# Both MLPs of a two-layer diffusion transformer with seven products of quarters in place of eight

## Chip, cores and metric

The kernel runs on one core of one Trainium2 chip, in one launch. The metric is the device time of that core in microseconds (us): the median of several executions. All arithmetic is fp32 in accuracy: each matrix product is made of three TensorE matmuls on operands split in a high and a low fp32r part (high x high, low x high, high x low).

## What is computed

Two blocks of a transformer over 256 prompt tokens and 1024 latent tokens, width 1024. Layer 0 mixes tokens with a state-space scan and gated linear attention, layer 1 with softmax attention. Behind each mixer stands an MLP of hidden width 4096 with a squared ReLU:

```python
def sq_relu_mlp(h, w1, w2):
    return jnp.square(jax.nn.relu(h @ w1)) @ w2
...
hp = modulate(rms_norm(yp, norm_mlp[i]), sp2, cp2)
hs = modulate(rms_norm(ys, norm_mlp[i]), sl2, cl2)
yp = yp + gp2 * sq_relu_mlp(hp, w_mlp_in[i], w_mlp_out[i])
ys = ys + gl2 * sq_relu_mlp(hs, w_mlp_in[i], w_mlp_out[i])
```

## The kernel before

Activations lie transposed, features on partitions: 8 tiles of 128 features by tokens. The tokens are three blocks: tb 0 and tb 1 are 512 latent tokens each, tb 2 is the 256 prompt tokens. A scheduler puts the instructions of each engine in an order of its own from the order in which the code issues them, and slower side work (the norms, the modulation vectors) is threaded into the main stream by `tick` and `drain`. Tiles come from pools and rings, and PSUM banks from a ring for each use (`ps`): whoever takes a bank or a slot waits for its last reader.

`mixer_out` finishes the mixer: for each of 8 output tiles m it multiplies by the output weights (`dense`, L406 to L408, three matmuls for each of the contraction's tiles), adds the gated result to x (`upd`, L1240) and sums squares for the norm. `norm` makes the columns of inverse roots and then, tile by tile, the normed activation and its high and low part (L1273 on DVE, L393 on ACT, L394 on DVE, L395 on POOL or DVE).

`mlp` goes over 16 slices of 256 hidden features. For each slice `up` makes two hidden tiles of each token block (8 contraction tiles by 3 matmuls at L406 to L408, squared ReLU on ACT at L1366 and L1367, the split by DVE L1368 and POOL L1369), and `down` multiplies them by the two rows of the second weight matrix for all 8 output tiles (L1383 to L1385), each result added to x at once by `upd` on DVE. A latent block's matmul has a moving operand of 512 columns, the prompt block's one of 256. Weights come as loads of 512 KB from SP's queue (`wload`, L240), are rounded to the high part on ACT (L241) and their low part is subtracted on POOL (L242).

The second layer's modulation vectors (`adaln`, L275) are computed inside the MLP of layer 0.

Of the kernel before, what the change touches and what calls it, by code (L numbers as in the profile page):

```python
# [33 lines left out]
class Arena:  # L34
# [339 lines left out]
def acts(h):  # L374
    return lambda k: (h[k // 4][0][k % 4], h[k // 4][1][k % 4])
# [727 lines left out]
def gla_second(s, hm):  # L1103
# [209 lines left out]
def mixer_out(s, l, w_src, key, part, h, ready, half=False):  # L1313


    acc = {}
    a, b = s.AB[key], s.mod[l][:, part]
    wsrc = w_src.rearrange("(k p) m -> p k m", p=128)

    def one(m, tb, w):  # L1320
        n = TBS[tb][1]
        if m == 0:
            acc[tb] = sums(s, tb)
        if half:
            p = dense(s, w, 4, lambda k: acts(h[tb])(4 + k), n, off=128 * (m % 2), ms=256)
        else:
            p = dense(s, w, KT, acts(h[tb]), n)
        upd(s, p, l, 2, m, tb, xk(s, tb, m), acc[tb])

    def load(m, eng=None):  # L1330
        if not half:
            s.wm = wload(s, wsrc[:, :, 128 * m:128 * m + 128], eng=eng)
        elif m % 2 == 0:
            s.wm = wload(s, wsrc[:, 4:8, 128 * m:128 * m + 256])
        return s.wm

    ready(0)
    for m in range(8):
        one(m, 0, load(m, s.nc.vector if m < 4 else None))
    ready(1)  # L1340
    for m in range(8):
        w = load(m)
        one(m, 1, w)
        if m == 0:
            norm_side(s, 0, acc[0], a, b, h)
        one(m, 2, w)
    return lambda tb: norm_side(s, tb, acc[tb], a, b, h)
# [679 lines left out]
```

## Time and profile before

| quantity | value |
|---|---|
| median of three runs | 3386.04 us (3375.12 to 3386.8) |
| profiled execution, its own time | 3382.89 us |
| its span from first to last instruction | 3381.1 us |
| mean granted TensorE clock | 0.973 |
| PE busy | 3208.6 us (95%) |
| DVE busy | 1709.7 us (51%) |
| ACT busy | 1035.0 us (31%) |
| POOL busy | 1053.1 us (31%) |
| mean DMA rate | 80 GB/s |

The span is the time that the rows below fill; the 1.8 us between it and the execution's own time lie around it. A PE that is 95% busy says that the matmuls set the time in most stretches. The MLPs lie from about 762 to 1727 us (layer 0) and from about 2480 to 3369 us (layer 1).

### The profile page before, as it was taken

To read this page: it belongs to the slowest core of one execution; us is meant where nothing else is said; L and a number is where in the kernel's file an instruction comes from. 1 tells how busy PE (TensorE), PEld (TensorE's weight loads), DVE (VectorE), ACT (ScalarE), POOL (GpSimd) and SP (SyncE) were. 2 spreads that over 40 slices of the span, in tenths; PEclk is the share of its full clock that TensorE was granted. 3 is DMA by queue.
4 is the path that set the end of the run, shared out by engine and by line. 5 is a ranking of instruction groups with operands and counts; after the bars stand their busy time and mean duration, and the time that the engine had idled before them with its cause. 6 is when DMAs were issued, how large, how long until landed. Compare 5 with 4: busy or idle time off the path is not lost.

```text
span 3381.1 us, 46292 instructions
## 1 busy us (share of the span) xinstructions
PE 3208.6 (95%) x18226; PEld 2686.9 (79%) x18226; DVE 1709.7 (51%) x3307; ACT 1035.0 (31%) x1911; POOL 1053.1 (31%) x828
## 2 busy tenths in 40 slices
PE   7987877999999999999999999999999999999999
PEld 4675546887787888888878888888878888888887
DVE  4576983647323333333367477775453434343333
ACT  4322322423121121111233277775322121212111
POOL 3443451135232222322244211112443232323231
PEclk9988888999999999999999999999999999999999
DMA  9432677522322221111122200102201111111111
GB/s 340 127 91 82 205 216 240 200 72 84 105 76 92 89 63 38 38 43 33 44 88 70 67 15 15 46 14 83 71 26 44 33 49 38 38 38 38 38 38 69
DMA packets 235562, 270.12 MB, mean 80 GB/s; under 512 B 32808, under 2 KB 185856, under 8 KB 229712
## 3 DMA queue, kind: packets, MB, share of 16 engines
q1 hardware_dynamic: 232208, 255.03, 24.3%
q0 software_dynamic: 3136, 12.13, 1.1%
q8 instruction: 143, 2.34, 0.3%
q14 instruction: 75, 0.61, 0.1%
HBM read 210.79 MB, written 56.33 MB: 79 GB/s over the span
## 4 chain that ended last, share of the span: by engine, by line
PE 76%; DVE 3%; ACT 1%; DMA 1%; issue 0%; POOL 0%; SPq 0%; ACTq 0%; DVEq 0%
PE banks L406 12%; PE banks L408 12%; PE banks L407 12%; PE banks L1383 9%; PE banks L1384 9%; PE banks L1385 9%; PE banks L1636 2%; PE banks L1600 1%; PE banks L1656 1%; PE banks L1657 1%; PE banks L1658 1%; PE banks L1601 1%; PE banks L1602 1%; PE banks L275 1%; DVE sb L394 1%; PE banks L1433 1%
## 5 line engine op out<-in xcount | busy, mean ns | idle before, releaser
L1240 DVE SCALAR_TENSOR_TENSOR sb<-banks,sb,sb 128x512 f32<-128x512 f32 (+1 forms) x840 | 552.4, 661 | 450.4 <-PE banks L1385 360.8
L242 POOL TENSOR_TENSOR sb_1024r<-sb,sb_1024r 128x1024 fp32r<-128x1024 f32 x178 | 429.2, 2419 | 1110.7 <-ACT sb_1024r L241 1088.2
L406 PE MATMUL banks<-sb_512r,sb_1024r 128*128 128x512 f32 x1664 | 661.3, 398 | 11.6 <-ACT sb_512r L393 5.8
L407 PE MATMUL banks<-sb_512r,sb_1024r 128*128 128x512 f32 x1664 | 658.1, 395 | 2.5 <-DVE sb_1024r L242 2.5
L408 PE MATMUL banks<-sb_512r,sb_1024r 128*128 128x512 f32 x1664 | 655.9, 396 | 4.6 <-DVE sb_512r L395 3.5
L241 ACT ACTIVATE sb_1024r<-sb 128x1024 fp32r<-128x1024 f32 x186 | 197.0, 1060 | 1062.0 <-DMA sb<-in_w_mlp_out 822.8
L1368 DVE CAST sb_512r<-sb 128x512 fp32r<-128x512 f32 x128 | 119.1, 930 | 593.2 <-ACT sb L1367 593.2
L1383 PE MATMUL banks<-sb_512r,sb_1024r 128*128 128x512 f32 x1024 | 405.1, 396 | 6.4 <-DVE sb_512r L1368 3.2
L1384 PE MATMUL banks<-sb_512r,sb_1024r 128*128 128x512 f32 x1024 | 400.9, 392 | 0.0
L1385 PE MATMUL banks<-sb_512r,sb_1024r 128*128 128x512 f32 x1024 | 396.6, 390 | 0.0
L406 PEld LDWEIGHTS banks<-sb_512r,sb_1024r 128*128 128x128 f32 x1664 | 317.3, 191 | 81.0 <-ACT sb_512r L393 8.2
L408 PEld LDWEIGHTS banks<-sb_512r,sb_1024r 128*128 128x128 f32 x1664 | 316.1, 190 | 81.3 <-DVE sb_512r L395 6.2
L407 PEld LDWEIGHTS banks<-sb_512r,sb_1024r 128*128 128x128 f32 x1664 | 317.2, 191 | 70.9 <-issue 5.9
L1383 PEld LDWEIGHTS banks<-sb_512r,sb_1024r 128*128 128x128 f32 x1024 | 193.3, 189 | 67.6 <-DVE sb L1240 16.3
L406 PE MATMUL banks<-sb_256r,sb_1024r 128*128 128x256 f32 x832 | 238.0, 286 | 2.6 <-DVE sb L1240 1.1
L408 PE MATMUL banks<-sb_256r,sb_1024r 128*128 128x256 f32 x832 | 237.5, 286 | 0.7 <-DVE sb_256r L395 0.6
L407 PE MATMUL banks<-sb_256r,sb_1024r 128*128 128x256 f32 x832 | 237.6, 286 | 0.0
L1369 POOL TENSOR_TENSOR sb_512r<-sb,sb_512r 128x512 fp32r<-128x512 f32 x128 | 165.4, 1292 | 223.2 <-DVE sb_512r L1368 223.2
L1385 PEld LDWEIGHTS banks<-sb_512r,sb_1024r 128*128 128x128 f32 x1024 | 192.7, 188 | 41.6 <-POOL sb_512r L395 0.8
L1366 ACT ACTIVATE sb<-banks 128x512 f32<-128x512 f32 (+1 forms) x192 | 100.5, 523 | 407.8 <-PE banks L408 383.4
L1384 PEld LDWEIGHTS banks<-sb_512r,sb_1024r 128*128 128x128 f32 x1024 | 193.4, 189 | 37.8
L406 PEld LDWEIGHTS banks<-sb_256r,sb_1024r 128*128 128x128 f32 x832 | 160.7, 193 | 8.0 <-DVE sb L1240 1.6
(359 smaller groups left out, 5661.9 us busy)
## 6 DMA issues: line engine op xcount, KB each, us to landing
sb<-in_w_ada SPq DMA_DIRECT2D x40, 1024.0 KB
sb<-in_w_mlp_in SPq DMA_DIRECT2D x64, 512.0 KB
sb<-in_w_mlp_out SPq DMA_DIRECT2D x64, 512.0 KB
sb<-in_w_in_e SPq DMA_DIRECT2D x16, 512.0 KB
xd<-sb SPq DMA_DIRECT2D x8, 1024.0 KB
sb<-in_w_ada SPq DMA_DIRECT2D x16, 512.0 KB
sb<-xd SPq DMA_DIRECT2D x8, 1024.0 KB
sb<-in_w_o_o SPq DMA_DIRECT2D x16, 512.0 KB
```

The source lines that it names most:

```text
L241: nc.scalar.activation(hi[:, :n], st[:, :n], AF.Copy)
L242: (eng or nc.gpsimd).tensor_tensor(lo[:, :n], st[:, :n], hi[:, :n].bitcast(F32), OP.subtract)
L406: nc.tensor.matmul(p[:mw, :n], hi[:, a:b], xh, start=(k == 0), stop=False)
L407: nc.tensor.matmul(p[:mw, :n], lo[:, a:b], xh, start=False, stop=False)
L408: nc.tensor.matmul(p[:mw, :n], hi[:, a:b], xl, start=False, stop=(k == kt - 1))
L1240: nc.vector.scalar_tensor_tensor(x, p[:, :n], s.mod[l][:, part, m, cnd:cnd + 1], x, OP.mult, OP.add)
L1366: nc.scalar.activation(r, p[:, :n], AF.Relu)
L1368: nc.vector.tensor_copy(mh, r)
L1369: nc.gpsimd.tensor_tensor(ml, r, mh.bitcast(F32), OP.subtract)
L1383: nc.tensor.matmul(p[:, :n], w2[j][0][:, ms], mh, start=(j == 0), stop=False)
L1384: nc.tensor.matmul(p[:, :n], w2[j][1][:, ms], mh, start=False, stop=False)
L1385: nc.tensor.matmul(p[:, :n], w2[j][0][:, ms], ml, start=False, stop=(j == 1))
```

## The change

Each MLP matrix product over the two latent blocks is seen as a product of 2 x 2 quarters: the weights in quarters A11, A12, A21, A22 (contraction half by output half), the activations in quarters by contraction half and token block. Eight products of quarters become seven, for which both sides need sums: four left factors S1 to S4 from each weight tile quadruple (`left_factors`), and seven right factors T from the activations. The prompt block, which has no partner, keeps plain products (`small_block`).

The sequence of one MLP is new too. `mixer_out` takes the blocks in the order (2, 0), then (1), and writes x back to DRAM (`x_close`); `norm_pair` makes h and T[0], T[4] from block 0, and later T[1], T[2], T[3], T[5], T[6] from block 1. `mlp_up` first goes over `SMALLS` = 5 steps of the prompt block and over two of seven products, A11 and A12, of `FIRST` = 3 steps; then over all 16 steps p (256 hidden features each). A step p >= 5 holds the prompt block's 48 matmuls of 256 columns and seven products of 12 matmuls of 512 columns. Its results are r11, r12, r21 and t; from them POOL makes the right factors for the second product, and eight tiles of 256 KB go to a DRAM buffer `md[p]`. `mlp_down` runs over 8 slices c of 512 hidden features (loading the T tiles from `md`) and in each over 4 pairs j of output tiles, with accumulators D in SBUF to which DVE adds each product from PSUM. At c = 7 it reloads x, makes the final sums (`out`) and the prompt block's last products come behind all others. `adaln` runs inside `mlp_down` of layer 0.

The weight ring holds 10 pairs of tiles [128, 512]; a step p takes 8 of them in the order A11, A12, A21, A22, S1, S3, S2, S4. Five PSUM banks serve the products; a step p >= 5 takes all five, so each name has the same bank in every step: A12 shares that of A11, A22 that of S1, S4 that of S3.

```diff
+PRODUCTS = (("A11", 0), ("S1", 1), ("S3", 2), ("S2", 3), ("A12", 0), ("A22", 1), ("S4", 2))
+def left_factors(s, A11, A12, A21, A22, S1, S2, S3, S4):
+
+    v = s.nc.vector
+    v.tensor_tensor(S1, A21, A22, OP.add)
+    v.tensor_tensor(S2, S1, A11, OP.subtract)
+    v.tensor_tensor(S3, A11, A21, OP.subtract)
+    v.tensor_tensor(S4, S2, A12, OP.subtract)
...
+def product(s, bank, w, off, step, B, first, last):
+
+    nc = s.nc
+    hi, lo = w
+    for k, (bh, bl) in enumerate(B):
+        o = slice(off + step * k, off + step * k + 128)
+        for i, (x, y) in enumerate(((hi, bh), (lo, bh), (hi, bl))):
+            nc.tensor.matmul(bank, x[:, o], y, start=first and k == 0 and i == 0,
+                             stop=last and k == len(B) - 1 and i == 2, skip_group_check=True)
+        tick(s, 0.68)
...
+def w_split(s, w, e):
+
+    hi, lo = w
+    raw = s.A.f32(lo)
+    s.nc.scalar.activation(hi, raw, AF.Copy)
+    e.tensor_tensor(lo, raw, hi.bitcast(F32), OP.subtract)
...
+def mlp_up(s, l, h, T, wr, tr):
...
+    def raw(p):
+        q = {}
+        for name, half, m in (("A11", 0, 0), ("A12", 1, 0), ("A21", 0, 1), ("A22", 1, 1)):
+            q[name] = wr()
+            c0 = 256 * p + 128 * m
+            nc.sync.dma_start(A.f32(q[name][1]).rearrange("p (a b) -> p a b", a=4),
+                              w1s[:, 4 * half:4 * half + 4, c0:c0 + 128])
+        return q
...
+        todo = ["A11", "A12"] * (p >= FIRST) + ["A21"] * (p >= SMALLS) + ["S1", "S3", "S2", "A22", "S4"]
+        for name in todo:
+            w_split(s, q[name], nc.gpsimd)
...
+            product(s, x, q[name], 0, 128, T[i], i < 4, i > 2)
+            if i < 4:
+                v.tensor_tensor(t, t, x, OP.add)
+            elif i == 5:
+                r21 = tr()
+                v.tensor_tensor(r21, t, x, OP.subtract)
+                rel(r21, r21)
+                nc.sync.dma_start(md[:, 2048:2560], r21)
+            else:
+                r12 = tr()
+                v.tensor_tensor(r12, t, x, OP.subtract)
+                rel(t, t)
+                nc.sync.dma_start(md[:, 3072:3584], t)
+                sq_relu(r12, r12)
+        g = nc.gpsimd
+        T1, T2, T4 = tr(), tr(), tr()
+        g.tensor_tensor(T1, r12, r11, OP.subtract)
+        nc.sync.dma_start(md[:, 512:1024], T1)
+        g.tensor_tensor(r12, t, r12, OP.subtract)
+        nc.sync.dma_start(md[:, 1024:1536], r12)
+        g.tensor_tensor(T2, t, T1, OP.subtract)
+        nc.sync.dma_start(md[:, 1536:2048], T2)
+        g.tensor_tensor(T4, T2, r21, OP.subtract)
+        nc.sync.dma_start(md[:, 2560:3072], T4)
...
+            for i, (name, b) in enumerate(PRODUCTS):
+                product(s, bank[b], *W[name], T[i], i < 4, i > 2)
+                if i < 4:
+                    add(d[3], bank[b], c == 0 and i == 0)
+                else:
+                    add(d[i - 4], bank[b], c == 0)
```

What stands in a row on the engines shows the move. On PE before, the seam between the prompt block's and a latent block's products of one `up` (the 256-column matmuls end, the next block's begin): each group waits at its first matmul for a bank, and a matmul for a weight part.

```order
L407 MATMUL banks<-sb_256r,sb_1024r 128x256
L408 MATMUL banks<-sb_256r,sb_1024r 128x256
L406 MATMUL banks<-sb_512r,sb_1024r 128x512 [waits DVE_49]
L407 MATMUL banks<-sb_512r,sb_1024r 128x512 [waits DMAHW4_49]
L408 MATMUL banks<-sb_512r,sb_1024r 128x512
```

On PE of the change, the seam between two steps p in the middle of `mlp_up`: the products A22 and S4 of a step, then the first matmul of the next step's prompt block, A11, S1, S2 and S3, in this order, and then the rest of the prompt block.

```order
L1452 MATMUL banks<-sb_512r 128x512 [waits DVE_49]
L1452 MATMUL banks<-sb_512r 128x512 x11
L1452 MATMUL banks<-sb_512r 128x512 [waits DVE_49]
L1452 MATMUL banks<-sb_512r 128x512 [waits Pool_49]
L1452 MATMUL banks<-sb_512r 128x512 x10
L1475 MATMUL banks<-sb_256r,sb_512r 128x256 [waits Activation_49]
L1452 MATMUL banks<-sb_512r 128x512 [waits Activation_49]
L1452 MATMUL banks<-sb_512r 128x512 [waits DVE_49,Activation_49]
L1452 MATMUL banks<-sb_512r 128x512 [waits Activation_49]
L1452 MATMUL banks<-sb_512r 128x512 [waits DVE_49]
L1476 MATMUL banks<-sb_256r,sb_512r 128x256 [waits DMAHW3_49,Pool_49]
```

The first matmul of S1 waits for DVE's r21 of the step before (its bank held A22), that of S3 for DVE's r12 (its bank held S4), and the prompt block's second matmul for POOL's low part of A11; everything behind them on PE waits with them.

On DVE of the change, the same seam: behind the step's last additions to t come the next step's S1, S3, S2 (L1439, L1441, L1440), r21 (L1571), S4 (L1442), the squared ReLU of r21 (L1489), r12 (L1576), that of t.

```order
L1439 TENSOR_TENSOR sb_512_6035<-sb_512_6031,sb_512_6033 128x512 [waits DMAHW1_49,DMAHW0_49,Pool_49]
L1441 TENSOR_TENSOR sb_512_6037<-sb_512_4272,sb_512_6031 128x512 [waits DMAHW3_49,PE_49]
L1440 TENSOR_TENSOR sb_512_6204<-sb_512_6035,sb_512_4272 128x512 [waits DVE_49]
L1571 TENSOR_TENSOR sb_512_3466<-sb_512_5434,banks 128x512 [waits DMAHW5_49,PE_49,Pool_49]
L1442 TENSOR_TENSOR sb_512_3472<-sb_512_6204,sb_512_6298 128x512 [waits DMAHW6_49,DVE_49]
L1489 SCALAR_TENSOR_TENSOR sb_512_3466<-sb_512_3466 128x512 [waits DVE_49]
L1576 TENSOR_TENSOR sb_512_3465<-sb_512_5434,banks 128x512 [waits DMAHW7_49,PE_49,Pool_49]
L1489 SCALAR_TENSOR_TENSOR sb_512_5434<-sb_512_5434 128x512 [waits DVE_49]
```

S1 to S4 are all made from loaded weights, and r21 and r12, which free PE's banks, stand behind S1, S3 and S2 (r12 behind S4 too) in DVE's row; before, DVE's row in the MLP held the additions to x (L1240) and six casts (L1368) for each slice.

On SP of the change, one step's DMAs (L1496 are weight loads: A11 of the step after the next, A22 of the next step, then A12 and A21 of the step after the next; the rest are stores to `md`):

```order
L1509 DMA md_5948<-sb_512_6029 128x512 [waits DMAHW2_49,Activation_49]
L1496 DMA sb_512_4274<-in_w_mlp_in 128x4x128 [waits DMAHW3_49,PE_49]
L1496 DMA sb_512_6033<-in_w_mlp_in 128x4x128 [waits DMAHW4_49,PE_49]
L1519 DMA md_5948<-sb_512_5431 128x512 [waits DMAHW5_49,Activation_49]
L1496 DMA sb_512_6208<-in_w_mlp_in 128x4x128 [waits DMAHW6_49,PE_49]
L1573 DMA md_5948<-sb_512_5432 128x512 [waits DMAHW7_49,DVE_49]
L1578 DMA md_5948<-sb_512_6030 128x512 [waits DMAHW0_49,DVE_49]
L1496 DMA sb_512_4272<-in_w_mlp_in 128x4x128 [waits DMAHW1_49,PE_49,Pool_49]
```

The load of A22 goes into the slot that the step before has used for A12, and waits for that product's last matmuls; before, SP's row held loads alone in the MLP, those of weights of 512 KB into a ring of five.

## Rows read from the trace of the kernel before

**Rows 1.** Windows: us, then engines busy (instructions), granted clock, DMA share, GB/s.
```profile
900.00:1000.00 100.00, 100.00 (x516) 78.79 (x516) 36.21 (x54) 16.32 (x24) 22.21 (x13) 1.00 0.30 95
1600.00:1700.00 100.00, 100.00 (x533) 86.65 (x532) 36.12 (x55) 20.26 (x32) 25.21 (x17) 1.00 0.14 40
2600.00:2700.00 100.00, 100.00 (x520) 86.09 (x519) 37.63 (x55) 18.57 (x29) 30.09 (x20) 1.00 0.11 32
700.00:900.00 200.00, 192.56 (x997) 154.77 (x996) 108.27 (x195) 63.80 (x100) 94.16 (x60) 0.99 0.25 81
1700.00:1800.00 100.00, 94.78 (x503) 79.97 (x502) 78.30 (x184) 40.64 (x67) 39.24 (x29) 0.97 0.23 79
2300.00:2600.00 300.00, 285.62 (x1562) 246.23 (x1561) 142.68 (x257) 100.59 (x168) 109.44 (x73) 0.98 0.20 60
```

**Rows 2.** Timeline of PE in a steady stretch: start, us, line, tile.
```profile
1182.03 0.28 PE L407 MATMUL banks<-sb_256r,sb_1024r 128*128 128x256 f32 x1
...
1182.63 0.40 PE L406 MATMUL banks<-sb_512r,sb_1024r 128*128 128x512 f32 x1
...
1185.83 0.39 PE L408 MATMUL banks<-sb_512r,sb_1024r 128*128 128x512 f32 x1
```

**Rows 3.** Costliest groups by shape: the matmuls that the change counts in.
```profile
L406 PE MATMUL banks<-sb_512r,sb_1024r 128*128 128x512 f32 x1664 | 661.3, 398 | 11.6 <-ACT sb_512r L393 5.8 <-DVE sb L1240 3.0 <-ACT sb_1024r L241 2.6
...
L1383 PE MATMUL banks<-sb_512r,sb_1024r 128*128 128x512 f32 x1024 | 405.1, 396 | 6.4 <-DVE sb_512r L1368 3.2 <-DVE sb L1240 3.1
```

**Rows 4.** Groups by shape, DVE, POOL and ACT: busy us, mean ns.
```profile
L1273 DVE TENSOR_TENSOR sb<-sb,banks 128x512 f32<-128x512 f32 x48 | 30.5, 678 | 4.4 <-PE banks L380 4.3
...
L962 DVE TENSOR_TENSOR sb<-sb,sb 128x512 f32<-128x512 f32 x8 | 5.4, 691 | 7.7 <-ACT sb L960 7.7
...
L1419 DVE TENSOR_TENSOR sb<-sb,sb 128x512 f32<-128x512 f32 x20 | 21.1, 1055 | 0.4
...
L394 DVE TENSOR_SCALAR sb<-sb,sb,sb 128x512 f32<-128x512 f32 x64 | 47.1, 762 | 1.6 <-ACT sb_512r L393 1.5
...
L1369 POOL TENSOR_TENSOR sb_512r<-sb,sb_512r 128x512 fp32r<-128x512 f32 x128 | 165.4, 1292 | 223.2 <-DVE sb_512r L1368 223.2
...
L395 POOL TENSOR_TENSOR sb_512r<-sb,sb_512r 128x512 fp32r<-128x512 f32 x48 | 71.3, 1501 | 97.5 <-DVE sb L394 77.7 <-DVE sb L209 14.2 <-DVE sb L205 3.6
...
L1366 ACT ACTIVATE sb<-banks 128x512 f32<-128x512 f32 x128 | 75.9, 593 | 289.9 <-PE banks L408 265.5 <-POOL sb_512r L1369 22.1 <-issue 2.3
...
L1367 ACT ACTIVATE sb<-sb 128x512 f32<-128x512 f32 x128 | 80.8, 632 | 4.0
```

**Rows 5.** Timeline of POOL and DVE with the layer-1 norm splits.
```profile
2481.32 1.53 POOL L1369 TENSOR_TENSOR sb_512r<-sb,sb_512r 128x512 fp32r<-128x512 f32 x1 [5.31 <-DVE sb_512r L1368]
...
2481.68 1.72 DVE L395 TENSOR_TENSOR sb_512r<-sb,sb_512r 128x512 fp32r<-128x512 f32 x1
...
2482.80 1.74 POOL L395 TENSOR_TENSOR sb_512r<-sb,sb_512r 128x512 fp32r<-128x512 f32 x1
```

**Rows 6.** A weight load of 512 KB: issue, and the ACT split behind it.
```profile
1298.25 0.38 SPq L240 DMA_DIRECT2D sb<-in_w_mlp_in  x1
...
1302.33 1.06 ACT L241 ACTIVATE sb_1024r<-sb 128x1024 fp32r<-128x1024 f32 x1 [3.10 <-DMA sb<-in_w_mlp_in]
```

**Rows 7.** Windows, columns as in the first group: gaps of PE and what followed.
```profile
2368.00:2371.50 3.50, 1.18 (x5) 0.41 (x4) 1.29 (x2) 1.06 (x1) 0.00 (x0) 1.00 0.48 145
2371.50:2374.90 3.40, 3.40 (x8) 2.72 (x9) 1.29 (x2) 1.58 (x2) 1.11 (x1) 0.50 0.05 15
2505.00:2508.00 3.00, 0.68 (x3) 0.21 (x2) 2.96 (x9) 3.00 (x7) 0.72 (x1) 1.00 0.00 0
2508.00:2511.40 3.40, 3.38 (x8) 2.73 (x9) 3.37 (x6) 1.63 (x4) 2.87 (x3) 0.50 0.00 0
762.00:782.00 20.00, 15.80 (x87) 13.06 (x86) 18.55 (x23) 8.84 (x14) 15.56 (x11) 1.00 0.15 41
```

More of the change, by code (lines that the diff above doesn't have):

```diff
@@ L1270, in norm @@
         col_bcast(s, p, rs[:, j:j + 1], j)
+    s.A.free(rs)
+    return p
+def norm(s, tb, acc, a, b, h):
+    nc = s.nc
+    n, cnd = TBS[tb][1], TBS[tb][2]
+    p = yield from norm_cols(s, tb, acc)
     for k in range(KT):
@@ L1310, in mixer_half, with mixer_out @@
                 upd(s, p, l, 2, 2 * j + i, tb, xk(s, tb, 2 * j + i))
-def mixer_out(s, l, w_src, key, part, h, ready, half=False):
-    acc = {}
+def mixer_out(s, l, w_src, key, part, h, ready):
+    nc, A = s.nc, s.A
     a, b = s.AB[key], s.mod[l][:, part]
     wsrc = w_src.rearrange("(k p) m -> p k m", p=128)
[L1320 to L1325, printed above, removed]
-        else:
[L1327 to L1347, printed above, removed]
@@ new lines, in mixer_out, with weights @@
+    T = [[] for _ in range(7)]
+    s.done -= {("h", 0), ("h", 1), ("h", 2), ("cols", 0), ("cols", 1)}
+    accs = [sums(s, tb) for tb in range(3)]
+    if l == 0:
+        kept = [wload(s, wsrc[:, 4:8, 256 * j:256 * j + 256], own=True) for j in range(4)]
+    def weights(m, first):
+        if l == 0:
+            w = kept[m // 2]
+            return lambda tb: dense(s, w, 4, lambda k: acts(h[tb])(4 + k), TBS[tb][1], off=128 * (m % 2), ms=256)
+        w = wload(s, wsrc[:, :, 128 * m:128 * m + 128], eng=nc.vector if first and m < 4 else None)
+        return lambda tb: dense(s, w, KT, acts(h[tb]), TBS[tb][1])
@@ new lines, in mixer_out @@
+    for tbs in ((2, 0), (1,)):
+        for tb in tbs:
+            ready(tb)
+        for m in range(8):
+            f = weights(m, tbs[0] == 2)
+            for tb in tbs:
+                upd(s, f(tb), l, 2, m, tb, xk(s, tb, m), accs[tb])
+                x_close(s, tb, m)
+        for tb in tbs:
+            if tb == 2:
+                norm_side(s, tb, accs[tb], a, b, h)
+            else:
+                side(s, norm_pair(s, tb, accs[tb], a, b, h, T))
+    A.free(kept) if l == 0 else w_free(s)
@@ new lines, in w_split, with small_block @@
+def w_split(s, w, e):
[3 more added lines that the diff above has]
+    e.tensor_tensor(lo, raw, hi.bitcast(F32), OP.subtract)
+def small_block(s, ws, offs, acts2):
+    nc = s.nc
+    V = ps(s, "mm")
+    for i in range(2):
+        o = V[:, 256 * i:256 * i + 256]
+        n = len(offs)
+        for k, (g, off) in enumerate(offs):
+            hi, lo = (x[:, off:off + 128] for x in ws[i][g])
+            xh, xl = acts2(k)
+            nc.tensor.matmul(o, hi, xh, start=(k == 0), stop=False)
+            nc.tensor.matmul(o, lo, xh, start=False, stop=False)
+            nc.tensor.matmul(o, hi, xl, start=False, stop=(k == n - 1))
+            tick(s, 0.36)
+    return V
@@ L1915, in layer0 @@
     A.free(used)
+    s.done.add("glu")
     for tb in range(3):
```

402 lines of the change are left out of this document (294 added, 108 removed).

## Prediction

> **What bounds the kernel now.** The page's busy shares and the windows by stage come first: PE is busy 95% of the span, and in the steady MLP stretches 100.00 of 100 us at granted clock 1.00 [rows 1]. There a matmul saved is time saved, and any wait that PE gets anew is time lost. Idle PE is at the seams only: 7.4 us of the 200 from 700, 5.2 of the 100 from 1700, 14.4 of the 300 from 2300 [rows 1]. DVE and POOL have room there, 36 to 38% and 22 to 30%.
>
> The timeline of PE gives the prices: from 1182.63 to 1185.83 lie 14 starts of 512-column matmuls, 0.2286 us each; five of 256 columns take from 1182.03 to 1182.63, 0.12 us each [rows 2]. The durations of some 0.4 us in the groups overlap and are no price [rows 3].
>
> **What the change removes.** Down, L1383 has 1024 matmuls of 512 columns, with L1384 and L1385 3072 [rows 3]; up, the loops make as many (16 slices x 2 tiles x 2 blocks x 8 x 3 x 2 layers), a part of L406's 1664 and its two neighbours' [rows 3]. Seven for eight of 6144 is 768 fewer; the prompt block's 256-column matmuls stay as many. The gain is 768 x 0.2286 = 175.6 us, if PE stays without waits. Everything else is what PE waits for anew.
>
> **The steady up step (p >= 5, 11 steps a layer).** Its PE work is 84 x 0.2286 + 48 x 0.12 = 25.0 us. At the seam, count from the end of product A12. PE still has A22 and S4 (24 x 0.2286 = 5.5 us) and the five first matmuls of the next step (1.0), 6.5 us in all. Meanwhile the next A22 load is issued, since its slot held A12. A load of 512 KB ran from issue at 1298.25 to the split at 1302.33, 4.1 us [rows 6]; half of it takes between 2.0 and 4.1, and I take 3.0, since part of it is latency. Then DVE goes down its row: S1, S3, S2, r21, S4, the squared ReLU of r21, r12, and only then has S3's bank on PE come free. Alone that is five operations of 0.69 us on SBUF operands (L962) and two of 0.68 with a PSUM operand (L1273) [rows 4], 4.8 us: r12 ends at 7.8, and with S3's first matmul PE goes on at 8.0, a stall of 1.5 us.
>
> But POOL splits A22, A21 and A11 in the same time, 1.29 us each (L1369) [rows 4], and DVE and POOL take turns. POOL's subtraction ends at 2482.85; DVE's, begun at 2481.68, ends at 2483.40, 0.55 us later; POOL's next ends at 2484.54, 1.14 us after DVE's [rows 5]. L1419, two SBUF operands beside a busy POOL, means 1.06 us [rows 4]. Four of DVE's SBUF operations (all but S1, before which POOL is idle) meet POOL. At 1.06 each r12 ends at 9.3, a stall of 3.0; followed turn by turn (A22's low part ends at 5.0, S3 5.5, S2 6.2, r21 6.9, A21's 7.4, S4 7.9, A11's 9.1, squared ReLU 9.6, r12 10.3) the stall is 4.0. I take 3.3, nearer to the mean of many. With the load's bounds it lies between 0.5 and 5.1. 22 steps x 3.3 = 73 us.
>
> The Trainium skill's page "SBUF — State Buffer", section "Who interferes with whom", speaks against the change here: a DVE instruction with two SBUF inputs contends with a GpSimd instruction that reads SBUF, and the one that comes later waits for the whole other. The trace agrees in kind; by the page DVE would end its full 0.69 us, not 0.55, behind POOL, in three places of the turns, or 22 x 0.4 = 9 us more for the two layers, an estimate that the sum does not use.
>
> **The clock.** At 2368, PE had two gaps with one matmul between them, 1.18 us busy of 3.5, and the next 3.4 us were granted 0.50, that is 1.2 instead of 2.4 GHz; after the gap at 2505 again [rows 7]. In the 20 us from 762, 4.2 us idle in shorter pieces left the clock at 1.00 [rows 7]. A stretch of 3.4 us at half speed costs 1.7. The seam leaves PE with two or three matmuls in some 5 us, like 2368; I take 1.4 a step (five steps in six), 31 us; bounds 0 and 37.
>
> **Steps 0 to 4.** Steps 0 to 2 hold 60 matmuls, 13.7 us; POOL has 9 operations and DVE 6 on SBUF, which in turn take 14.0 (pairs of 1.69) to 15.7: 1.2 us late each. Steps 3 and 4 take four banks of five, so S3's bank waits for r21, not r12: 2.2 with the clock. 8 a layer, 16 us (5 to 22).
>
> **Start of the MLP.** While `norm_pair` makes the factors of block 1, PE has five small blocks and six products, 5 x 5.76 + 72 x 0.2286 = 45 us. DVE has 28 operations for the factors and 10 early splits, POOL 16 and 10: in turn 26 x 1.69 and 12 DVE more at 0.69, 52 us; step 0's own splits add 8, the norm's columns some 5. The last factor is wanted 11 us into step 0, at 56: 9 late, a layer. Before lost some 16 us at the same place (part of the 7.4 and 14.4 above), so the net is about 5 us over both layers (-10 to 25).
>
> **Down.** A pair j is 42 x 0.2286 + 24 x 0.12 = 12.5 us, a slice c 50. POOL has 25 splits (32 us), DVE 7 splits and 16 half-size left factors (10), 43 of 50 in turn; the 32 PSUM additions (22 us) take no turn. The left factors are made a whole j ahead, and S4's bank is freed by one addition: PE bounds. I take 0.5 us for each of 14 slices, 7 us (0 to 42). The first T tiles are loaded behind the last stores: 2 us (0 to 8). At c = 7 DVE has the final sums and x besides, some 12 us for PE's 9.6 a pair, of which five banks and the prompt products behind take most: 6 us (3 to 12).
>
> **End of layer 0.** Both latent norms now start behind c = 7. Eight tiles at 0.68 + 0.76 + 1.50 (L1273, L394, L395 [rows 4]) are 23 us a block, beside 11.5 us of prompt products and then block 0's first four groups of the next projection, 22 us, which follow tile by tile. Before, this seam lost 5.2 us [rows 1]. I take 8 more (2 to 18). The adaln matmuls, x's store and reload and the stores to `md` (twelve transfers of 256 KB in some 28 us, 110 GB/s, where the 100 us from 900 ran at 95 with PE full [rows 1]) cost nothing: SP and the DMA engines are off PE's path, and if a store held A22's load, the seam above would grow by as much.
>
> **Sum.** 73 + 31 + 16 + 5 + 7 + 2 + 6 + 8 = 148 us lost of 175.6: 28 gained. The profiled execution took 3382.9 us, 3 below the median, so 3355 there and 3358 as a median. The measurement tells no change from about 0.5%, 17 us.
>
> **Rivals.**
> (a) *The seam is covered.* DVE does not wait for POOL there and PE keeps its clock: 22 x 1.5 = 33 and nothing for the clock, 77 lost in all, 3288. For it: shorter gaps left the clock alone [rows 7], and POOL's share at a seam is not that of rows 5. Against it: rows 5, where each operation of the kind waited.
> (b) *Full turns at each seam.* 4.0 + 1.7 = 5.7 a step, 125 us instead of 104: 3379, no measurable change. For it: rows 5 and 7 taken at their word. Against it: L1419's mean.
> (c) *Slower, by the change of c.* The ring holds 20 T tiles and a slice takes 14, so T[3] on is loaded as the last j frees it. From its landing, 3 us after A11 of j = 3, to S4 of the next slice are 16 us; 8 T splits, 2 of the prompt block and those of two pairs are 14 on POOL and 12 on DVE, of which 8 half-size, 18 + 5.6 us in turn: 7 late, 14 times, 98 instead of 7 us: 3449. It decides from (28 + 17) / 14 = 3.2 us a slice. Against it: the weights' parts are made a pair ahead, and that lead can be spent first.
>
> **Chances.** The forecast 0.38 (its own range 3335 to 3380: 0.26 faster, 0.12 the same), (a) 0.22, (b) 0.20 (0.13 the same, 0.07 slower), (c) 0.20. Together faster 0.48, same 0.25, slower 0.27. The range 3275 to 3435 leaves out the outer part of (a) and of (c).
>
> **What would show it.** PE at about 5376 and 3072 MLP matmuls; in the windows of the up part about 25 of every 30 us busy, at a mean clock near 0.95, each gap ended by DVE (r12, L1576), with POOL's L1462 close behind; in the down part PE near 100. Wrong would be: gaps ended by a load (then the ring is the cause), by POOL alone (then the splits bound), or PE at 99% in up, or idle at each change of c.

## The result and the profile after

The changed kernel takes 3469.49 us (median, 3465.76 to 3471.65), the kernel before 3385.7 in the same runs: a ratio of 1.0253, 95% interval 1.0231 to 1.0276. It is 2.5% slower. The forecast was 3358 with a range of 3275 to 3435, so the time lies outside, on the side to which I gave 0.27.

The page's busy line of the change:

```profile
PE 3111.0 (90%) x17458; PEld 2589.2 (75%) x17458; DVE 2096.6 (60%) x3643; ACT 1328.4 (38%) x2485; POOL 1647.6 (47%) x1306
```

This one line splits the loss. Before, PE was busy 3208.6 of 3381.1 us and idle 172.5; now it is busy 3111.0 of 3469.9 and idle 358.9. The 768 matmuls are gone (5376 products and 3072 of the prompt block remain), and should have made busy time fall by 175.6 us; it fell by 97.6. So **78 us went into matmuls that ran slower (the mean granted clock is 0.943 where it was 0.973), and 186 us into new idle time**: 78 + 186 - 175.6 = 88.8, the whole growth of the span. The forecast had 31 and 117 for the two.

The windows of the change by stage (columns as in [rows 1]): all ahead of the first MLP, the start of each MLP while `norm_pair` works (797 and 2528.8), steps 0 to 4, steps 5 to 15, slice c = 0, c = 1 to 6, c = 7; for layer 0 the stretch to attention and attention too; last the tail.

```profile
0.00:767.00 767.00, 636.08 (x4090) 494.27 (x4091) 488.40 (x1032) 235.81 (x431) 276.21 (x269) 0.90 0.57 173
767.00:797.00 30.00, 25.83 (x121) 21.23 (x120) 26.13 (x65) 16.20 (x28) 11.20 (x11) 0.94 0.35 115
797.00:867.00 70.00, 49.17 (x308) 44.59 (x307) 64.00 (x62) 35.42 (x64) 50.15 (x32) 0.83 0.31 94
867.00:957.50 90.50, 85.22 (x377) 69.48 (x377) 42.04 (x52) 29.91 (x50) 62.16 (x45) 0.98 0.45 146
957.50:1287.00 329.50, 292.94 (x1453) 247.58 (x1452) 120.81 (x129) 105.83 (x177) 198.91 (x140) 0.95 0.35 117
1287.00:1349.50 62.50, 56.42 (x290) 44.37 (x289) 35.46 (x42) 32.33 (x58) 48.25 (x35) 0.95 0.65 219
1349.50:1679.50 330.00, 327.93 (x1767) 262.00 (x1766) 219.56 (x329) 113.94 (x193) 199.17 (x146) 1.00 0.54 178
1679.50:1743.30 63.80, 56.39 (x282) 46.72 (x281) 60.45 (x82) 20.15 (x32) 30.43 (x22) 0.95 0.58 174
1743.30:1978.30 235.00, 211.41 (x1122) 181.23 (x1121) 128.60 (x303) 73.88 (x129) 74.23 (x52) 0.91 0.18 58
1978.30:2405.40 427.10, 411.36 (x2810) 367.51 (x2808) 308.85 (x772) 297.34 (x709) 74.27 (x117) 0.98 0.09 26
2405.40:2528.80 123.40, 105.48 (x538) 89.60 (x536) 62.71 (x97) 37.63 (x58) 51.91 (x35) 0.93 0.42 126
2528.80:2594.00 65.20, 50.05 (x310) 45.52 (x311) 52.23 (x50) 35.03 (x64) 43.97 (x29) 0.83 0.33 100
2594.00:2679.50 85.50, 83.03 (x372) 67.80 (x372) 42.54 (x52) 29.13 (x49) 59.34 (x44) 1.00 0.47 151
2679.50:3010.00 330.50, 293.67 (x1453) 248.14 (x1452) 119.07 (x132) 106.82 (x179) 197.44 (x139) 0.95 0.35 118
3010.00:3071.00 61.00, 54.41 (x266) 45.28 (x265) 33.25 (x39) 32.04 (x57) 48.38 (x36) 0.94 0.49 164
3071.00:3384.00 313.00, 303.15 (x1586) 258.82 (x1584) 228.00 (x326) 112.39 (x189) 198.40 (x147) 0.99 0.37 118
3384.00:3447.80 63.80, 56.82 (x292) 47.33 (x291) 56.19 (x77) 10.09 (x18) 23.20 (x17) 0.95 0.29 88
3447.80:3469.90 22.10, 11.65 (x55) 7.73 (x54) 8.35 (x15) 4.52 (x8) 0.00 (x0) 0.68 0.65 225
```

Stages of before: all ahead of the first MLP, the MLP of layer 0, the three that answer to 1743, 1978 and 2405, and the MLP of layer 1:

```profile
0.00:762.00 762.00, 636.77 (x4073) 495.44 (x4074) 492.02 (x1044) 240.89 (x434) 283.16 (x269) 0.90 0.57 175
762.00:1727.50 965.50, 957.89 (x4990) 791.55 (x4989) 384.34 (x597) 208.27 (x318) 296.97 (x189) 1.00 0.21 67
1727.50:1939.90 212.40, 204.75 (x1148) 176.83 (x1146) 128.04 (x292) 70.99 (x127) 79.28 (x53) 0.98 0.21 65
1939.90:2359.60 419.70, 407.86 (x2781) 362.11 (x2781) 306.33 (x763) 299.10 (x711) 76.42 (x119) 1.00 0.10 29
2359.60:2480.00 120.40, 114.47 (x604) 98.05 (x603) 48.79 (x80) 38.10 (x53) 58.05 (x33) 0.99 0.26 80
2480.00:3369.00 889.00, 880.58 (x4601) 758.62 (x4600) 346.29 (x529) 174.06 (x267) 259.18 (x166) 0.99 0.13 38
```

Length less PE's busy time is the idle time of a stage: in steps 5 to 15, 36.6 and 36.8 us; at the start 20.8 and 15.2. Even attention, which the change does not touch, took 7 us longer: 4 of them idle time, the rest at a clock of 0.98 where it had 1.00.

What PE waited for in steps 5 to 15, first in layer 0 and then in layer 1 (releaser, us, times, longest; a wait for several semaphores is put to the one that came last):

```profile
PE banks L1452 <- DVE sb L1576: 27.9, 11, 2.6
PE banks L1452 <- ACT sb_512r L1461: 8.6, 10, 1.8
```

```profile
PE banks L1452 <- DVE sb L1576: 28.2, 11, 2.6
PE banks L1452 <- ACT sb_512r L1461: 8.6, 11, 2.1
```

In first place stands r12, the subtraction whose end frees S3's bank, as forecast: 56.1 of 73.3 us. The other 17.2 are waits for ACT's rounding of S2, which starts when DVE has made S2 (L1440); these the forecast did not name. One seam of it, on SP's queue, DVE and PE (timelines: start, us, engine, line):

```profile
1100.34 3.10 SPq L1496 DMA_DIRECT2D sb<-in_w_mlp_in  x2
```

```profile
1105.94 0.69 DVE L1439 TENSOR_TENSOR sb<-sb,sb 128x512 f32<-128x512 f32 x1 [4.69 <-DMA sb<-in_w_mlp_in]
1106.55 0.68 DVE L1441 TENSOR_TENSOR sb<-sb,sb 128x512 f32<-128x512 f32 x1
1107.16 1.79 DVE L1440 TENSOR_TENSOR sb<-sb,sb 128x512 f32<-128x512 f32 x1
1108.87 0.67 DVE L1571 TENSOR_TENSOR sb<-sb,banks 128x512 f32<-128x512 f32 x1
1109.46 1.16 DVE L1442 TENSOR_TENSOR sb<-sb,sb 128x512 f32<-128x512 f32 x1
1110.55 1.75 DVE L1489 SCALAR_TENSOR_TENSOR sb<-sb 128x512 f32<-128x512 f32 x1
1112.22 0.68 DVE L1576 TENSOR_TENSOR sb<-sb,banks 128x512 f32<-128x512 f32 x1
```

```profile
1109.69 0.70 PE L1452 MATMUL banks<-sb_512r 128*128 128x512 f32 x2 [0.64 <-ACT sb_512r L1461]
1112.95 0.51 PE L1452 MATMUL banks<-sb_512r 128*128 128x512 f32 x1 [2.56 <-DVE sb L1576]
```

DVE stands still until the load of A22 has landed, 2.5 us after its issue (the second of the two, done at 1100.34 + 3.10); from S1's start to r12's end are 7.0 us, with three of the SBUF operations stretched from 0.7 to 1.2 to 1.8 us beside POOL; PE waits 0.6 us (for the high part of S2) and 2.6 (for r12). That is the chain of the forecast (3.0 for the load, 6.3 to 7.3 for the row, a stall of 3.0 to 4.0), with each link of about the forecast size.

### The profile page after: what moved, and what is told of

It is laid out like the page before. It is cut to its first block, busy times and chain, and to the rows that moved or that the text cites. A ratio compares the mean times of both kernels' runs of the same rounds, so it can differ in the third digit from the quotient of the medians.

```text
span 3469.9 us, 48829 instructions
## 1 busy us (share of the span) xinstructions
PE 3111.0 (90%) x17458; PEld 2589.2 (75%) x17458; DVE 2096.6 (60%) x3643; ACT 1328.4 (38%) x2485; POOL 1647.6 (47%) x1306
## 5 line engine op out<-in xcount | busy, mean ns | idle before, releaser
L1452 PE MATMUL banks<-sb_512r 128*128 128x512 f32 x5376 | 1316.1, 399 | 127.3 <-DVE sb L1576 60.8
L1452 PEld LDWEIGHTS banks<-sb_512r 128*128 128x128 f32 x5376 | 1015.8, 193 | 376.8 <-DVE sb L1576 71.0
L1462 POOL TENSOR_TENSOR sb_512r<-sb,sb_512r 128x512 fp32r<-128x512 f32 x654 | 926.6, 1445 | 630.1 <-issue 199.9
L1461 ACT ACTIVATE sb_512r<-sb 128x512 fp32r<-128x512 f32 x786 | 478.0, 628 | 844.8 <-DMA sb<-in_w_mlp_in 203.0
L1646 DVE TENSOR_TENSOR sb<-sb,banks 128x512 f32<-128x512 f32 x472 | 318.8, 683 | 171.4 <-PE banks L1452 153.4
L404 PE MATMUL banks<-sb_512r,sb_1024r 128*128 128x512 f32 x640 | 263.3, 412 | 28.4 <-ACT sb_1024r L236 10.5
L1568 DVE TENSOR_TENSOR sb<-sb,banks 128x512 f32<-128x512 f32 x96 | 65.9, 686 | 333.0 <-PE banks L1452 324.6
L405 PE MATMUL banks<-sb_512r,sb_1024r 128*128 128x512 f32 x640 | 260.1, 407 | 0.5 <-DVE sb_1024r L237 0.5
L406 PE MATMUL banks<-sb_512r,sb_1024r 128*128 128x512 f32 x640 | 257.9, 404 | 1.9 <-POOL sb_512r L393 1.1
L237 POOL TENSOR_TENSOR sb_1024r<-sb,sb_1024r 128x1024 fp32r<-128x1024 f32 x46 | 111.7, 2429 | 200.3 <-ACT sb_1024r L236 158.7
L1462 DVE TENSOR_TENSOR sb_512r<-sb,sb_512r 128x512 fp32r<-128x512 f32 x132 | 152.3, 1155 | 57.1 <-ACT sb_512r L1461 55.9
L1476 PE MATMUL banks<-sb_256r,sb_512r 128*128 128x256 f32 x512 | 152.3, 297 | 26.6 <-DVE sb_512r L1462 26.5
L404 PEld LDWEIGHTS banks<-sb_512r,sb_1024r 128*128 128x128 f32 x640 | 125.3, 196 | 60.2 <-ACT sb_1024r L236 10.7
L1475 PE MATMUL banks<-sb_256r,sb_512r 128*128 128x256 f32 x512 | 152.8, 299 | 0.9 <-ACT sb_512r L1461 0.9
L1475 PE MATMUL banks<-sb_512r 128*128 128x256 f32 x512 | 147.0, 287 | 6.6 <-DVE sb L1646 4.5
L1477 PE MATMUL banks<-sb_256r,sb_512r 128*128 128x256 f32 x512 | 152.5, 298 | 0.0
L406 PEld LDWEIGHTS banks<-sb_512r,sb_1024r 128*128 128x128 f32 x640 | 124.4, 194 | 35.8 <-POOL sb_512r L393 3.8
L405 PEld LDWEIGHTS banks<-sb_512r,sb_1024r 128*128 128x128 f32 x640 | 125.2, 196 | 31.5 <-issue 6.1
L1477 PE MATMUL banks<-sb_512r 128*128 128x256 f32 x512 | 145.7, 285 | 0.9 <-POOL sb_512r L1462 0.9
```

The costliest lines, as they stand in the source:

```text
L404: nc.tensor.matmul(p[:mw, :n], hi[:, a:b], xh, start=(k == 0), stop=False)
L405: nc.tensor.matmul(p[:mw, :n], lo[:, a:b], xh, start=False, stop=False)
L406: nc.tensor.matmul(p[:mw, :n], hi[:, a:b], xl, start=False, stop=(k == kt - 1))
L1452: nc.tensor.matmul(bank, x[:, o], y, start=first and k == 0 and i == 0, stop=last and k == len(B) - 1 and i == 2, skip_group_check=True)
L1461: s.nc.scalar.activation(hi, raw, AF.Copy)
L1462: e.tensor_tensor(lo, raw, hi.bitcast(F32), OP.subtract)
```

## The experiments

"Excess" below is the length of a stretch less its matmuls at full speed (512 columns 0.2286 us, 256 columns 0.12), so it holds idle time and half clock together; two numbers with a bar are layer 0 and layer 1. In the change, steps 5 to 15 had 54.9|55.9 (11 x 24.96 = 274.6 us of work in each), the start 25.2|20.5, c = 0 7.1|11.1, c = 7 12.3|11.4. The kernel before took 3378.2 to 3383.5 us beside these runs.

### Does the slot of A22 or the bank of r12 make the steady loss?

Theory 1: the seam stalls because A22's load has to wait for A12's slot. Rival: five banks are too few, and r12 would be late for S3 anyway. The first edit changes the order in which a step takes its slots to A21, A22, A11, A12: in the ring of ten, A21 and A22 then get those of S2 and S4 of two steps before, long free, and A12, which is needed only fifth, that of A22 of the step before. The second gives the up part all eight banks; the third is both.

```diff
-        q = raw(p)
+        q = raw(p, (2, 3, 0, 1))
```

> The up steps take the ring's slots in the order A21, A22, A11, A12, S1, S3, S2, S4 instead of A11, A12, A21, A22, ..., so that the load of the next A22 no longer waits for product A12 (the early part keeps its order). Theory 1 (the chain at the seam begins with the late load and ends with r12): S1 and S2 are made during the step, a step falls from 29.8 to about 26.5 us, 22 steps gain 70 us, some 3400 us. Theory 2 (POOL and DVE taking turns bound the step, whenever the load comes): steps stay above 29 us, the gain is below 15 us.

Measured: 3368.34 us, 0.9977 of before (0.9965 to 0.999), 101 less than the change. A window of its steps 5 to 15:

```profile
1000.00:1100.00 100.00, 100.00 (x532) 86.45 (x532) 41.55 (x45) 35.28 (x60) 64.80 (x48) 1.00 0.39 127
```

PE has no gap left and full clock: the excess fell to 3.8|3.1, a step to 25.3 us, so that the gain is 31 more than the 70 that theory 1 had put. DVE and POOL do the same work in the same steps, so in these steps their turns cost nothing by themselves; they did only behind a late load.

```diff
+            was = s.bk["mm"]
+            s.bk["mm"] = tuple(range(8))
```

> From step 0 on the up products use all eight PSUM banks in turn instead of five, so that S3's first matmul does not wait for r12 of the step before. Theory 1: r12 is the last link of the chain, but POOL's low part of A11 stands some 1 us before it, so a step falls by 1 us only, 29.8 to about 28.8, 20 to 25 us in all, some 3447 us, and the gaps are then ended by POOL's or DVE's split of A11. Rival (the bank alone is the cause): a step falls by 4 us, 85 us in all.

Measured: 3465.96 us, 1.0261 (1.0231 to 1.0291); excess of the steps 58.8|59.8. No gain, but the run does not isolate the bank. With five banks of eight taken in turn, r21's bank comes to the prompt block of the step after the next, and r12's to that step's product A11. PE waits for just these two at the seam, so the scheduler has put those first matmuls one whole step further ahead, and in the steps of layer 0 PE waited for r12 as before (24.7 us in nine places; 27.9 in eleven in the change) and for r21 besides:

```profile
PE banks L1452 <- DVE sb L1578: 24.7, 9, 2.7
PE banks L1475 <- DVE sb L1573: 5.0, 9, 1.1
```

> Slot order of the first and eight banks of the second together. Theory 1: nothing of the seam is left but POOL's splits, which are made during the step; steps at 25.0 to 25.8 us, full clock through the up part, 88 to 105 us less than the changed kernel, 3365 to 3382 us. Theory 2 (turns bound): steps stay above 28 us.

Measured: 3378.36 us, 1.0 (0.999 to 1.001), 10 more than with the slots alone; excess of the steps 4.9|6.6. Theory 1 holds: with the load early, the steady loss is gone; whether free banks would have done it too stays untried, since no order was run in which the bank alone was free. The next runs, up to the versions on DVE, stand on the version with new slot order.

### What bounds the start of the MLP?

In the start's windows, 797 to 876, PE waited longest for one of the two early splits that stand on DVE (waits: releaser, us, times, longest):

```profile
PE banks L1476 <- DVE sb_512r L1462: 11.7, 1, 11.7
PE banks L1452 <- DVE sb_512r L1305: 8.0, 1, 8.0
```

That split stood behind seven of `norm_pair`'s (timelines of DVE and, below, POOL):

```profile
847.95 11.80 DVE L385 TENSOR_TENSOR sb_512r<-sb,sb_512r 128x512 fp32r<-128x512 f32 x7
859.68 1.74 DVE L1462 TENSOR_TENSOR sb_512r<-sb,sb_512r 128x512 fp32r<-128x512 f32 x1
```

```profile
854.16 6.71 POOL L385 TENSOR_TENSOR sb_512r<-sb,sb_512r 128x512 fp32r<-128x512 f32 x4
```

So I first moved the early splits off DVE (in the change as it was, not with the new slots). Theory: the place in DVE's row costs the 11.7 us. Rival: the turns bound the start, and the wait only moves.

```diff
-            w_split(s, q[name], nc.vector if i % 2 else nc.gpsimd)
+            w_split(s, q[name], nc.gpsimd)
```

> In the five early steps all four weight splits go to POOL instead of every second to DVE. Theory A (the wait of 11.7 and 14.8 us in the early part is that of a weight split which stands in DVE's row behind seven splits of the factors): these waits go, and with them some of the low clock, 25 to 40 us less, some 3437 us. Theory B (DVE and POOL in turn have too much to do before step 0, whoever does it): the wait moves to POOL's row and the gain is below 10 us.

Measured: 3470.64 us, 1.0277 (1.0251 to 1.0304). The start fell from 25.2|20.5 to 23.1|11.0, but layer 1's steps 0 to 4 rose from 3.2 to 13.7: the rival. Two more runs press the same question from both sides: less early work on PE, and less work for DVE and POOL.

```diff
-SMALLS, FIRST = 5, 3
+SMALLS, FIRST = 5, 1
```

> From here on the first experiment's slot order (e1_slot, 3368 us) is the base. FIRST = 1: only step 0's A11 and A12 come early, steps 1 and 2 do theirs later, so PE has 11 us less of its own work while the factors of block 1 are made. Theory A (before step 0, DVE and POOL taking turns are the bound, and PE's early work is only cover): what is taken from the early part is not filled, 15 to 22 us more over both layers, some 3386 us. Rival (PE waits there for one weight split in the wrong place, whatever it has to do): within 5 us of the base.

Measured: 3393.05 us, 1.0042 (1.0025 to 1.006), 25 more than its base. The first products of the steps 1 and 2 are cover: taken out of the start, PE waits there instead (39.0|34.8, counted over the same 72 matmuls of products as in the others, 48 of which are step 0's own here).

```diff
         hi, lo = h1(k + 4)[0], A.r(x1[k])
-        split(s, hi, lo, x1[k], k)
+        nc.scalar.activation(hi, x1[k], AF.Copy)
...
-            product(s, x, q[name], 0, 128, T[i], i < 4, i > 2)
+            product(s, x, q[name], 0, 128, [(hi, lo) for (hi, _), (_, lo) in zip(T[i], T[1])], i < 4, i > 2)
```

> Base e1_slot; the low parts of the factors T[2], T[3], T[5] and T[6] are not computed (16 subtractions a layer, eight on DVE, eight on POOL), the products take that of T[1] in their place. Theory A (turns at 1.7 us a pair bound the start): 8 pairs less, 9 to 13 us a layer, 18 to 26 us in all, some 3346 us. Rival (the chain from the norm's columns to the first factor bounds it): below 6 us.

Measured: 3338.5 us, 0.9879 (0.9851 to 0.9908), 30 less than its base; the start fell to 11.9|6.5, which is 27 of the 30. The element work of the start is what bounds it: with less of it the start is shorter.

### What does slice c = 7 wait for?

PE waited up to 4.4 us there for an addition of DVE (L1646, L1648 with the new slots). Theory: for the last slice the weights' slots come from a second place (`own`), so all its left factors are made in one burst in front of the additions. Rival: DVE is simply full. The first edit makes the slots go around as in every other slice; the second drops the deferral, so that each pair j has its prompt products behind it.

```diff
         s12, s34 = wr(), wr()
+        if own:
+            wr(), wr()
```

> Base e1_slot; at the last slice of the down part each pair takes two more slots of the weight ring and leaves them unused, so that the left factors are made two and a half pairs ahead as in the other slices, not all four pairs at once. Theory (at c = 7 the left factors of all four pairs stand in DVE's row ahead of the addition that frees PE's bank, 4.4 us and a stretch of low clock): the wait goes, 4 to 6 us a layer, 8 to 12 us in all, some 3358 us. Rival (DVE has the same work either way, and is late at the end instead): below 3 us.

Measured: 3370.3 us, 0.997 (0.9958 to 0.9981); c = 7 had 13.0|11.1. But the edit did not move what it was to move. Every engine has its instructions in the same order as in the base, and the burst of left factors still stands in DVE's row, from 1627.75 to the addition (L1650 here) on which PE waits (its last two operations and the addition, then PE):

```profile
1631.80 1.48 DVE L1439 TENSOR_TENSOR sb<-sb 128x256 f32<-128x256 f32 x1
1633.21 1.48 DVE L1441 TENSOR_TENSOR sb<-sb,sb 128x256 f32<-128x256 f32 x1
1634.61 0.67 DVE L1650 TENSOR_TENSOR sb<-sb,banks 128x512 f32<-128x512 f32 x1
```

```profile
1635.34 28.49 PE L1452 MATMUL banks<-sb_512r 128*128 128x512 f32 x118 [4.54 <-DVE sb L1650]
```

So this run is its base once more (3368.34 and 3370.3), and decides nothing between theory and rival. The rows speak for the theory: here as in the change (1686.25 to 1693.11, a wait of 4.0 us) six left factors in one row stand ahead of the addition.

```diff
-            own = [Tr() for _ in range(6)] + [T2r() for _ in range(2)]
...
-            else:
-                small(c, j, w, U)
+            small(c, j, w, U)
...
-        small(7, j, w, U)
```

> Base e1_slot; the prompt block's products of the last slice stand in their pairs as in the other slices, not behind all of them. Theory (they cover the norms behind layer 0's MLP and the last outputs): c = 7 itself loses some 8 us less a layer, but the seam behind it loses its cover, 8 to 11 us more; in sum -5 to +8 us against 3368. Rival (the deferral is what makes c = 7 slow and covers nothing): 15 to 20 us less.

Measured: 3351.3 us, 0.991 (0.9885 to 0.9936): 17 less than its base (its four executions took 3338.8 to 3353.8). The excess of c = 7 is gone (0.0|0.1). From the last MLP matmul of layer 0 to the start of attention it is 240.8 us, with the deferral 240.9 (235.0 in the change itself). The deferred products covered nothing of the norm behind them; behind layer 1's MLP they did cover something, since the last stretch is 27.2 us without the deferral and 22.3 with it. Why c = 7 got free is not settled: the second place for the slots went with the deferral, and in DVE's row the burst is gone, its left factors in four groups; that the products in their pairs, 24 matmuls each, give DVE the time for its additions is argued. What follows c = 7 stays dear, in this version as in the change:

```profile
1640.00:1669.00 29.00, 29.00 (x155) 24.96 (x153) 27.32 (x38) 8.41 (x12) 13.23 (x8) 1.00 0.60 172
1669.00:1720.00 51.00, 35.17 (x156) 29.86 (x155) 46.59 (x96) 22.07 (x34) 17.82 (x15) 0.77 0.37 120
```

PE full up to 1669, then 35 of 51 us at a clock of 0.77 while DVE is busy 47 of them.

### Is one engine better than two in turns?

If the turns bound the start, DVE alone might be faster than both: two subtractions on DVE 1.38 us, a pair in turns 1.7. Base is the version above. First `norm_pair`'s and the early splits' work all on DVE:

```diff
-    v, g = nc.vector, nc.gpsimd
+    v = g = nc.vector
...
-            w_split(s, q[name], nc.vector if i % 2 else nc.gpsimd)
+            w_split(s, q[name], nc.vector)
```

> Base: the first experiment's slot order with the last slice's prompt products not deferred (f3_nodefer, 3351 us). All that norm_pair and the early weight splits gave to POOL goes to DVE. Theory (a pair of operations in turn takes 1.70 us, two on DVE alone 1.38): the early part, 25 and 21 us above its matmuls, loses 6 to 12 us a layer, 12 to 24 in all, some 3333 us. Rival (POOL's work is help, and DVE alone has too much): slower than the base by 10 us or more.

Measured: 3327.88 us, 0.9853 (0.9838 to 0.9868), 23 less than its base (19 by the two ratios) and **the fastest version: 1.5% under the kernel before**. Its start has 9.9|7.3 where the base has 24.7|20.6, 28 less; 10 of these come back in steps 0 to 4 (11.9|6.8 for 3.8|4.5). In the start's window of layer 0 and on DVE inside it:

```profile
797.00:853.00 56.00, 49.37 (x324) 44.56 (x323) 46.08 (x85) 35.22 (x64) 3.29 (x2) 0.97 0.41 127
```

```profile
838.70 1.89 DVE L385 TENSOR_TENSOR sb_512r<-sb,sb_512r 128x512 fp32r<-128x512 f32 x3
840.51 0.68 DVE L1334 TENSOR_TENSOR sb<-sb,sb 128x512 f32<-128x512 f32 x1
```

POOL is idle, and DVE starts an operation each 0.60 us (three in 1.81 from start to start): a pair 1.20, less than I had put.

```diff
-                w_split(s, w, nc.gpsimd if n % 2 else v)
+                w_split(s, w, v)
```

> Base f3_nodefer; in the down part all seven splits of T that went to POOL go to DVE. Theory: the first pair of a slice, 14.6 us for 12.5 in layer 1, comes nearer to 12.5, and the first slice's burst is shorter, 5 to 10 us a layer, some 3337 us. Rival (DVE's additions, which free PE's banks, now stand behind more splits): no change or slower.

Measured (base again the version without deferral): 3362.44 us, 0.9951 (0.9931 to 0.9971), 11 more. In the down part of layer 0, 1240 to 1640, PE now waits 10.8 us in five places for an addition, 3.2 in two places in the base; here DVE frees the banks, and what stands in its row delays them.

> Both, and also the low parts of the other norms on DVE alone. Theory: the two gains add, and the seam behind layer 0 (three norms with no cover) loses 3 to 6 us more, some 3320 us. Rival: the sum is smaller than the parts or turns to a loss, since POOL stands idle where DVE is the bound.

Measured (both, and the norm's low parts on DVE too): 3337.37 us, 0.9881 (0.9866 to 0.9896), 9 more than the first of the two alone.

### What does slice c = 0 wait for?

The first slice keeps 11.2|14.2 in the fastest version. Theory A: the first left factors stand behind 18 T tiles on SP's queue. Theory B: the slots bind.

```diff
+        W0 = load_w(0, 0) if c == 0 else None
         T, U = load_T(c)
...
-            W, w = load_w(c, j)
+            W, w = W0 if c + j == 0 else load_w(c, j)
```

> Base: the version with the ring order changed, the prompt block's products in their pairs and the start's element work on DVE (3327.88 us; excess of slice c = 0 over its matmul work 11.2 us in layer 0 and 14.2 in layer 1). Edit: the first weight quadruple of the second product is loaded ahead of slice 0's 18 T tiles instead of behind them. Theory A: the first slice waits for its left factors because their loads stand behind the burst of T tiles in SP's queue; then the excess of c = 0 falls to about 4 to 8 us a layer, and the time by 8 to 18 us, to 3310 to 3320. Theory B: the loads of the left factors wait for ring slots that the last up step's own products hold (7.8 us of SP's waits for PE in this place), so SP's queue stands still with the T tiles behind the weight load; then c = 0 keeps 10 to 20 us a layer and the time stays within 5 us or grows, 3325 to 3345.

Measured: 3328.2 us, 0.983 (0.9808 to 0.9852), the same; c = 0 has 8.9|13.6. This edit moved nothing either: every engine has its instructions in the order of the base. There the scheduler had already put the first loads of the down part's weights (L1632) ahead of the T tiles (L1615) on SP:

```profile
1190.78 0.38 SPq L1632 DMA_DIRECT2D sb<-in_w_mlp_out  x1
1199.17 0.39 SPq L1632 DMA_DIRECT2D sb<-in_w_mlp_out  x1
1202.51 1.34 SPq L1615 DMA_DIRECT2D sb<-md  x3
```

So A's premise does not hold in this version, by the rows and not by the run, and B was not tried. The run is the fastest version once more (3327.88 and 3328.2). In the change as it was, PE's waits in c = 0 of layer 0 are for r12 (3.0 us) and r21 (2.6) of the last up step, 5.6 of 6.1 us idle; both stand in DVE's row behind splits of T tiles (L1462, from 1287.81 on). In layer 1 r12 has 1.4 of 6.6, and the rest is spread. A third thing at this seam is the DMA engines' share (second number from the right), here in the fastest version:

```profile
1212.00:1229.00 17.00, 12.72 (x56) 9.96 (x54) 11.08 (x13) 11.40 (x21) 12.90 (x9) 0.97 0.95 311
```

All 16 DMA engines are busy there. Whether they bind was not tried.

## Why the prediction was wrong, point by point

**The gain** of 175.6 us was there: the steps at full clock take 25 us.

**The steady up step was right.** Idle 36.6 + 36.8 = 73.4 us against 73. That close, it is in part luck: at the seam shown the load took 2.5 us for my 3.0, the row 7.0 at the upper end of 6.3 to 7.3, and 17 us of the idle time are the waits for S2's high part, which my chain did not have. Slower matmuls there: 292.94 + 293.67 less 2 x 274.6 is 37 us, against 31. The mechanism was right, and the slot run shows that the late load is its root: with the load early, all of it goes. Rival (a), the covered seam, is out, and (b), full turns, had it too high. The Trainium skill's page "SBUF — State Buffer", section "Who interferes with whom", has a DVE instruction with two SBUF inputs contend with a GpSimd instruction that reads SBUF, and calls the shared ports an exclusive lock. The rows agree in kind, with a pair of turns at 1.68 us ((859.68 - 847.95) / 7, in the start); if each waited for the whole of the other, a pair would be 0.60 + 1.29 = 1.89 (DVE alone in the fastest version, POOL alone in [rows 4]).

**The start of the MLP failed: a net of 5 us.** Idle is 36.0 us in the two starts, and 7.0 more in a wait for ACT's rounding of a weight (L1461) at the first product of layer 1: 43 where I had 18. Ahead of them idle time grew as well, for which I had nothing: by 5 in layer 1 (2405 to 2529, 17.9 with those 7.0, against 5.9 before) and by 10 in layer 0 (0 to 797, 135.1 against 125.2 up to 762 before). With the 16 that before lost in its MLPs taken off (7.6 and 8.4, windows of before above), that is a net of some 42. The step that failed is the balance of 65 us of DVE's and POOL's work, 52 of it in turns, against 56 of PE's. It summed the whole start; but PE does not wait at its end alone. In layer 0 it waits at the first product for T[0] (8.0 us, L1305), and at the first early split for the row ahead of it (11.7; 14.8 in layer 1), and PE's later work cannot cover these. The runs bear this out: less early work on PE costs 25 (FIRST = 1), less element work gains 30 (no low parts), the same work on DVE alone gains 23, and moving the early splits alone gains nothing.

Of what lies ahead, 10.5 us in layer 1 is PE's wait for a split (ACT L236) of an output projection's weight, whose load stands on SP behind the reloads of x (L1363, at 2402.81). I had put x's store and reload at nothing; that they cost this is read from the rows, and no run tried it. In layer 0, 4.2 of the 10 is the projection's wait for the additions to x (L1241); the rest stays open.

**Slices 0 to 6 failed: 7 + 2 us.** Idle is 12.7 in c = 0 and 11.9 in c = 1 to 6. For c = 0 I had taken SP's order as the only limit, "behind the last stores"; in layer 0 PE waited there for r21 and r12, put off by splits of T tiles in DVE's row. The slice changes of rival (c) did not come in layer 0, where c = 1 to 6 has 2.1 us idle in 330. In layer 1 they came, a quarter of the size: 9.9 idle, with a wait at each of the five changes (an addition L1646 4.5 us in all, ACT's L1461 4.7), some 1.8 a change where (c) had 7. The outcome was slower, but mostly by other ways than (c).

**c = 7 was mis-sized: 6 us**, measured 14.4 idle. The step said that the five banks and the deferred prompt products take DVE's surplus; the run without the deferral, and so without the second place for the slots, has none left. In the rows the wait stands behind a burst of six left factors, which that step did not count.

**The end of layer 0 was mis-sized: 8 us.** The idle time from there to attention grew from 7.7 to 23.6. All three norms do start behind c = 7, as I had said. Of the 23.6, 11.0 are PE's waits for the norms' columns (6.0 at L378, 5.0 at L1258), of which before had none at this place; I had counted the work tile by tile alone. No run tried it. Attention and the tail, at which I had put nothing, lost 4 and 5 more of idle time.

**The clock was priced in one place only.** 31 us was right for the steps, but of 78 us, 41 came elsewhere: the stretches with the misjudged waits have a low clock too (0.83 at both starts, 0.91 behind layer 0's MLP, 0.68 in the tail). This is the largest single part of the miss of 117 us (3471.65 against 3355 in the profiled execution): clock 47, start 37, slices 0 to 6 16, c = 7 8, end of layer 0 8, tail and attention 9, less 8 for steps 0 to 4, which had 8 of idle time where I gave 16.

**Open**: what c = 0 waits for in layer 1 and whether the DMA engines' rate has a part in it; whether the burst or the place of the prompt products made c = 7 wait; and, read from rows alone, the 16 us behind layer 0's MLP and what lies ahead of the two starts.

## What to carry to other kernels

When a change takes matmuls away from a PE that is nearly full, write down for each seam which load, slot and bank the first matmuls behind it need, and see that no load waits for a slot which the product just ahead of the seam still reads: here the order of four names in a ring was worth 101 us. See in the trace that an edit has moved what it was to move: two of the edits above left every engine's row as it was. Add up busy and idle time of PE apart, since waits cost twice, once as idle time and again as half clock behind them, and price the clock at every stall, not at the steady ones alone. Two engines that take turns at SBUF can be slower than one of them alone, as in the start of the MLP, but not where that one also frees the banks, as in the down part.

## What was not expected of the hardware

A chain of DVE subtractions on SBUF operands, alone, runs at 0.60 us each, and in turn with POOL a pair takes 1.68: POOL's help made the start longer. The squared ReLU (L1489), which reads one SBUF tile, is stretched beside POOL as well: 1.75 us at the seam. In the change's attention, with the same work as before, the clock was 0.98 where it had been 1.00. At the turn from up to down of the fastest version the DMA engines were busy for 95% of 17 us at 311 GB/s, in a kernel whose mean is 130 GB/s.
